# The z projection of a hybrid decoder layer, with its hi products 512 columns wide

## The chip, the cores and the metric

The kernel runs on one core of one Trainium2 chip. The metric is the device time of one execution in microseconds; for the kernel before, three runs gave 731.35, 731.69 and 731.74 us, median 731.69. Differences are read in one further execution that the hardware profiler recorded.

The engines have short names in the profile: PE is the matrix engine (TensorE; PEld is its weight loads), DVE is VectorE, ACT is ScalarE, POOL is GpSimd, SP issues most of the transfers. Each engine takes its instructions in one fixed order and stops at the first one whose inputs are not there. SBUF is the on-chip memory, 128 partitions wide; PSUM is the memory into which PE accumulates, in banks of 128 x 512 float32.

## The reference, cut to what matters

```python
# x: (1, 256, 1024) float32; one layer
h = h + 0.5 * rmsnorm(swiglu(rmsnorm(h, g1), w_gate1, w_up1, w_down1), p1)
u = rmsnorm(h, mix_pre_g)
z, xbc, dt_raw, q, k, v, gate_logits = jnp.split(u @ w_in, IN_SPLITS, axis=-1)   # z: 2048 columns
y_ssd = ssd_branch(z, xbc, dt_raw, ...)      # ... y = y * silu(z), then a grouped rmsnorm and a product
y_att = diff_attn_branch(q, k, v, ...)
h = h + rmsnorm((gates[0] * y_ssd + gates[1] * y_att) @ w_out, mix_post_g)
h = h + 0.5 * rmsnorm(swiglu(rmsnorm(h, g2), w_gate2, w_up2, w_down2), p2)
```

The change touches how `z = u @ w_in[:, 0:2048]` is computed. `z` is needed only at `silu(z)`, after the state-space branch (SSD) has its `y`.

## The kernel before, in words

All products are made in float32r, in which each operand is split into a rounded `hi` part and a rest `lo`, and three of the four partial products are added: hi·hi, hi·lo and lo·hi. The weights stream from HBM in chunks of 1 MB (`raw`, three buffers). For each chunk ACT casts two halves to `whi` (L259) and DVE subtracts to make two halves of `wlo` (L260), two or three chunks ahead of PE.

The normalized input `u` lies transposed in SBUF with 256 tokens: its hi part `ah`, its lo part `al`, and the two side by side in 512 columns as `ahl`.

**The z stage** is the loop at L1517 to L1523. It takes eight weight chunks of 1024 x 256, two for each of four groups g, so `pz00`, `pz01`, `pz10` ... `pz31`; the text below also calls them c0 to c7. For each chunk `mm_t` (L323) writes both 128-row halves m of the result into the two halves of one PSUM bank (`pjt`, of three banks `pj`): per half, 16 matmuls with `whi` as the stationary operand, alternately on `ah` (L330) and `al` (L331), then eight with `wlo` on `ah` (L333), all of 256 columns. Then ACT copies the bank to `sz` (L1522). After the stage ACT applies Silu to `sz`.

The stages next to it (`xs` ahead, `q` and `k` behind) use `mm_w` (L355) on chunks of the same shape. There each half m has a bank of its own: eight matmuls of 512 columns with `whi` on `ahl`, so that hi·hi lands in columns 0 to 255 and hi·lo in 256 to 511, and eight of 256 columns with `wlo` on `ah` into columns 0 to 255 (`mm_part`, L341). Then ACT copies the right half of the bank to SBUF and DVE adds the left one (`taken_from`, L347 and L348).

**Work woven into the z stage.** `back.run(BG_US)` behind each chunk feeds steps of `ssd_work` (L1246). For each group g: PE transposes `xs` (`px`, L1252), DVE scales it to `X` (L1253); for each half hf of the group, a transfer issued on POOL's queue brings the tile `acb` (cumulated decays, broadcast to 128 partitions, L1262); from it ACT and DVE build two tiles `E` (ACT: eight passes over 128 columns and one exp over 512, in the helper `act`, L415; DVE: L1269, and a product with the mask tile, L1274). With all four `E` of a group PE makes `py` (32 matmuls, L1284), in the order 3, 2, 1, 0, so the first `py` matmul needs the last `E`. DVE adds `py` into `xs` (L1291).

**What sets the order.** In this stage no order is written by hand: the framework's scheduler places each engine's instructions at build time from its own estimates, and the chip then keeps that order. POOL's queue holds, around this stage, only the eight `acb` transfers. Buffers: `k4` 29 of 4 KB (weights, `acb`, `sz`), `k2` 7 of 2 KB, `k3` 4 (`E`).

Of the kernel before, what the change touches and what calls it, by code (L numbers as in the profile page):

```python
# [19 lines left out]
ALU = mybir.AluOpType  # L20
# [6 lines left out]
P = 128  # L27
T = 256
# [26 lines left out]
def tile_hybrid_layer(ctx: ExitStack, tc: tile.TileContext, x, ffn1_pre_g, ffn1_w_gate, ffn1_w_up,  # L55
# [4 lines left out]
    nc = tc.nc  # L60
# [5 lines left out]
    def k4(shape, name, dt=F32):  # L66
        return sb.tile(shape, dt, tag="k4", name=name, bufs=K4_BUFS)
# [4 lines left out]
    def k2(shape, name, dt=F32):  # L72
        return sb.tile(shape, dt, tag="k2", name=name, bufs=K2_BUFS)
# [7 lines left out]
    def pj(name):  # L81

        return ps.tile([P, 512], F32, tag="pj", name=name, bufs=3)

    def pjt(name):

        return pj(name).rearrange("p (m t) -> p m t", m=2)

    def bg(shape, name):
        return ps.tile(shape, F32, tag="bg", name=name, bufs=5)  # L90
# [197 lines left out]
    def split_to(n):  # L288

        while len(splits) < min(n, len(units)):  # L290
            of, p = units[len(splits)]
            if p is not None:
                splits.append(of.split(p))
                continue
            for _ in split_steps():
                pass

    def ahead_of(i, n):

        n *= 4  # L300
        while n > 0 and i < len(units):
            n -= 4 if units[i][1] is None else 1
            i += 1
        return i

    def take(ahead=AHEAD):

        i = taken[0]
        taken[0] += 1
        split_to(ahead_of(i, ahead))  # L310
        (of, p), w = units[i], splits[i]
        splits[i] = None
        if p is not None:
            return w
        his, los = w
        nj = chunks[of][1][1] // 2
        return (lambda j: his[j // nj][:, j % nj, :], lambda j: los[j // nj][:, j % nj, :])
# [5 lines left out]
    def mm_t(acc, w, act, k0=0, first=True, last=True, ks=range(KD)):  # L323

        (wh, wl), (ah, al, _) = w, act
        acc = acc if isinstance(acc, list) else [acc[:, m, :] for m in range(2)]
        for m in range(2):
            cs = slice(m * P, (m + 1) * P)
            for j in ks:
                nc.tensor.matmul(acc[m], wh(j)[:, cs], ah(k0 + j), start=first and j == ks[0], stop=False)  # L330
                nc.tensor.matmul(acc[m], wh(j)[:, cs], al(k0 + j), start=False, stop=False)  # L331
            for j in ks:
                nc.tensor.matmul(acc[m], wl(j)[:, cs], ah(k0 + j), start=False, stop=last and j == ks[-1])  # L333

    def mm_part(acc, w, act, m, part, first):


        (wh, wl), (ah, _, ahl) = w, act
        to, w_, x_ = (acc, wh, ahl) if part == "hi" else (acc[:, :T], wl, ah)
        for j in range(KD):  # L340
            nc.tensor.matmul(to, w_(j)[:, m * P:(m + 1) * P], x_(j), start=first and j == 0,  # L341
                             stop=not first and j == KD - 1, skip_group_check=True)

    def taken_from(acc, dst, scale=None):

        if scale is None:
            nc.scalar.copy(dst, acc[:, T:])  # L347
            nc.vector.tensor_tensor(dst, acc[:, :T], dst, ALU.add)  # L348
        else:
            nc.scalar.activation(dst, acc[:, T:], AF.Copy, scale=scale)  # L350
            nc.vector.scalar_tensor_tensor(dst, acc[:, :T], scale, dst, ALU.mult, ALU.add)

    PARTS = (("hi", "lo"), ("lo", "hi"))
# [9 lines left out]
    def mm_runs(dst, name, w, act, n):  # L363


        banks = [pj(f"{name}{m}") if n % 2 == 0 else bg([P, 512], f"{name}{m}") for m in range(2)]
        for part in PARTS[n % 2]:
            for m, acc in enumerate(banks):
                mm_part(acc, w, act, m, part, part == PARTS[n % 2][0])
                if part == PARTS[n % 2][1]:  # L370
                    taken_from(acc, dst[:, m, :])

    def mm_nat(acc, w, act, k0, first, last, late):


        (wh, wl), (ah, al) = w, act
        pairs = [(ah, wh), (al, wh), (ah, wl)] if late == "w" else [(ah, wh), (ah, wl), (al, wh)]
        terms = [(p, j) for j in range(4) for p in pairs[:2]] if late == "w" else \
            [(p, j) for p in pairs[:2] for j in range(4)]
        terms += [(pairs[2], j) for j in range(4)]  # L380
        for i, ((a, b), j) in enumerate(terms):
            nc.tensor.matmul(acc, a(k0 + j), b(j), start=first and i == 0, stop=last and i == 11)  # L382
# [112 lines left out]
    def new_u(tag):  # L495
        for i in range(2):
            uT[i] = sb.tile([P, 4, 2, T], F32R, tag="u8", name=f"u{i}_{tag}", bufs=2)

    act_u = (lambda j: uT[j // 4][:, j % 4, 0, :], lambda j: uT[j // 4][:, j % 4, 1, :],
             lambda j: uT[j // 4][:, j % 4, :, :])  # L500
# [370 lines left out]
    def ffn(post_v, tag, ready, turned, then, products):  # L871
# [28 lines left out]
        for j in range(2, FF // T):  # L900
            if j % 2 == 0:
                gh = k4([P, 4, T], f"gh_{tag}{j}", F32R)
                gl = k4([P, 4, T], f"gl_{tag}{j}", F32R)
            o = (j % 2) * 2
            gu += [(gh[:, o + m, :], gl[:, o + m, :]) for m in range(2)]
            sg = k2([P, 2, T], f"sg_{tag}{j}")
            mm_runs(sg, f"pg_{tag}{j}", take(), act_u, 0)
            act(sg, sg, AF.Silu)
            su = k2([P, 2, T], f"su_{tag}{j}")
            mm_runs(su, f"pup_{tag}{j}", take(), act_u, 1)  # L910
            nc.vector.tensor_tensor(sg, su, sg, ALU.mult)  # L911
            split(gh[:, o:o + 2, :], gl[:, o:o + 2, :], sg)
            if j // 2 in QUADS[tag]:
                if j % 2:
                    sums[j // 2] = sums_of(j // 2, even, sg)
                else:
                    even = sg
# [304 lines left out]
    for i in range(4):  # L1222
        acc = k2([P, 2, T], f"bc{i}")
        mm_w(acc, f"pbc{i}", take(), act_u)
        dst = (bT, cT)[i // 2]
# [16 lines left out]
    sz = [None] * 4  # L1242
# [265 lines left out]
    for g in range(4):  # L1508
        xs[g] = k4([P, 4, T], f"xs{g}")
        for i in range(2):  # L1510
            acc = k2([P, 2, T], f"xr{g}{i}")
# [5 lines left out]
    for g in range(4):  # L1517
        sz[g] = k4([P, 4, T], f"sz{g}")
        for i in range(2):
            acc = pjt(f"pz{g}{i}")  # L1520
            mm_t(acc, take(), act_u)
            nc.scalar.copy(sz[g][:, i * 2:i * 2 + 2, :], acc)  # L1522
            back.run(BG_US)  # L1523
    act_table(SILU)
    for g in range(4):
# [94 lines left out]
    acc = [[bg([P, 512], f"acc_mx{b}{q}") for q in range(2)] for b in range(2)]  # L1620
# [50 lines left out]
```

## Time and profile before

| | |
|---|---|
| median of three runs | 731.69 us |
| the profiled execution | 731.22 us, its span 729.3 us |
| busy, share of the span | PE 99%, PEld 85%, DVE 83%, ACT 65%, POOL 4% |
| xs stage | 237.9 to 285.3 us of the span |
| z stage | 285.3 to 340.0 us |
| q and k stage | 339.9 to 392.0 us |
| `acb` transfers issued on POOL | at 278.59, 284.86, 301.98, 302.94, 317.86, 323.24, 339.79, 346.96 us |

How to read it. The span goes from the first to the last instruction; the profiled execution's own time is 1.92 us longer. A row of a timeline has the start, the duration, engine, line, operation, output<-inputs, shape and count, and in brackets how long the engine stood idle before it and what ended that. Rows of consecutive instructions overlap by some hundredths of a microsecond to a tenth, since the next instruction enters the pipeline before the last one has left; the step from one start to the next is the price in a full queue. Matmuls are pipelined, so that their rows show 0.28 us or 0.39 us for one while the next begins after 0.12 us; the chain of waits shows the step.

### The profile page before, as it was taken

What the parts mean: (1) busy time and instruction counts of PE and PEld (TensorE: products, weight loads), DVE (VectorE), ACT (ScalarE), POOL (GpSimd) and SP (SyncE); (2) the same over time, 40 slices, a digit from 0 to 9 for tenths busy, and PEclk for the clock granted to TensorE, in tenths of its full rate; (3) what the DMA queues carried; (4) which work ended last, traced back from release to release, by engine and by line L of the source; (5) the groups of instructions that cost most, each with busy time, mean ns of one, the idle gap of its engine ahead of it and who ended that gap; (6) DMA issues with size and microseconds to landing.
All of it is one profiled execution on the core that took longest, in us unless ns stands there. A gap on an engine that the chain in (4) does not pass through costs nothing.

```text
span 729.3 us, 10568 instructions
## 1 busy us (share of the span) xinstructions
PE 721.3 (99%) x4025; PEld 620.5 (85%) x4025; DVE 608.5 (83%) x933; ACT 472.8 (65%) x804; POOL 31.5 (4%) x63
## 2 busy tenths in 40 slices
PE   9999999999999999999999999999999999999996
PEld 8888888888778889999888788888888888888885
DVE  6978788999979989777996998785784878789996
ACT  6657666666867676869965577782563756566562
POOL 4300000000200000000000000000010000000000
PEclk9999999999999999999999999999999999999998
DMA  8884654467674557665564664465461655654551
GB/s 303 229 275 153 208 173 176 170 231 260 185 227 119 172 173 238 208 213 180 155 224 147 205 224 137 152 235 199 120 234 51 230 182 166 231 194 156 174 197 58
DMA packets 94450, 137.92 MB, mean 189 GB/s; under 512 B 2668, under 2 KB 68800, under 8 KB 94400
## 3 DMA queue, kind: packets, MB, share of 16 engines
q1 hardware_dynamic: 91728, 129.51, 53.7%
q0 software_dynamic: 2368, 7.22, 3.3%
q8 instruction: 31, 0.51, 0.3%
q10 hardware_dynamic: 304, 0.53, 0.2%
q14 instruction: 19, 0.16, 0.1%
HBM read 136.17 MB, written 1.08 MB: 188 GB/s over the span
## 4 chain that ended last, share of the span: by engine, by line
PE 95%; DVE 2%; DMA 1%; issue 1%; ACT 0%; DVEq 0%; ACTq 0%
PE pup_f L341 14%; PE pg_f L341 14%; PE pxs L341 6%; PE pws L382 6%; PE pgt L382 6%; PE acc_f2p L755 5%; PE acc_f1p L755 3%; PE pbc L341 3%; PE pk L341 3%; PE pq L341 3%; PE pn_f L398 3%; PE acc_mx L676 3%; PE pn_mx L382 3%; PE pn_f L382 3%; PE pwd L382 3%; PE pz L333 2%
## 5 line engine op out<-in xcount | busy, mean ns | idle before, releaser
L260 DVE TENSOR_TENSOR wlo<-raw,whi 128x1024 fp32r<-128x1024 f32 x216 | 257.0, 1219 | 20.2 <-ACT whi L259 19.0
L259 ACT CAST whi<-raw 128x1024 fp32r<-128x1024 f32 x216 | 218.4, 1049 | 16.1 <-DMA raw<-in_w_in_dram 5.7
L341 PE MATMUL pg_f<-u_f,whi 128*128 128x512 f32 x288 | 69.0, 390 | 0.0
L341 PE MATMUL pup_f<-u_f,whi 128*128 128x512 f32 x288 | 68.7, 391 | 0.0
L341 PEld LDWEIGHTS pg_f<-u_f,whi 128*128 128x128 f32 x288 | 53.9, 188 | 11.1
L341 PEld LDWEIGHTS pup_f<-u_f,whi 128*128 128x128 f32 x288 | 52.9, 188 | 10.2
L130 ACT CAST wqh<-wt 128x1024 fp32r<-128x1024 f32 x24 | 25.2, 1055 | 23.5 <-DVE wt L122 23.4
L341 PEld LDWEIGHTS pg_f<-u_f,wlo 128*128 128x128 f32 x288 | 36.9, 191 | 1.4
L341 PE MATMUL pup_f<-u_f,wlo 128*128 128x256 f32 x288 | 37.5, 283 | 0.0
L341 PE MATMUL pg_f<-u_f,wlo 128*128 128x256 f32 x288 | 37.4, 283 | 0.0
L347 ACT COPY su_f<-pup_f 128x256 f32<-128x256 f32 x36 | 13.2, 372 | 36.1 <-PE pup_f L341 36.1
L341 PEld LDWEIGHTS pup_f<-u_f,wlo 128*128 128x128 f32 x288 | 35.9, 192 | 0.0
L348 DVE TENSOR_TENSOR su_f<-pup_f,su_f 128x256 f32<-128x256 f32 x36 | 15.2, 421 | 24.2 <-ACT su_f L347 24.1
L382 PE MATMUL pgt<-whi,u_mx 128*128 128x512 f32 x128 | 33.1, 393 | 0.0
L341 PE MATMUL pxs<-u_mx,whi 128*128 128x512 f32 x128 | 31.8, 394 | 0.0
L330 PE MATMUL pz<-u_mx,whi 128*128 128x256 f32 x128 | 31.6, 284 | 0.0
L331 PE MATMUL pz<-u_mx,whi 128*128 128x256 f32 x128 | 31.5, 283 | 0.0
L136 DVE TENSOR_TENSOR wql<-wt,wqh 128x1024 fp32r<-128x1024 f32 x24 | 29.1, 1217 | 0.2
L382 PEld LDWEIGHTS pgt<-whi,u_mx 128*128 128x128 f32 x128 | 23.6, 188 | 5.3 <-issue 0.7
L341 PEld LDWEIGHTS pxs<-u_mx,whi 128*128 128x128 f32 x128 | 23.2, 189 | 4.3
L320 ACT CAST gh_f<-sg_f 128x512 fp32r<-128x512 f32 x18 | 11.2, 620 | 23.2 <-DVE sg_f L911 23.2
L136 DVE TENSOR_TENSOR wql<-raw,wqh 128x1024 fp32r<-128x1024 f32 x18 | 21.8, 1219 | 3.5 <-ACT wqh L130 3.5
(415 smaller groups left out, 1585.1 us busy)
## 6 DMA issues: line engine op xcount, KB each, us to landing
raw<-in_w_in_dram SPq DMA_DIRECT2D x40, 1024.0 KB, 5.1
raw<-in_ffn_w_down_dram SPq DMA_DIRECT2D x22, 1024.0 KB, 4.9
raw<-in_ffn_w_gate_dram SPq DMA_DIRECT2D x20, 1024.0 KB, 5.4
raw<-in_ffn_w_up_dram SPq DMA_DIRECT2D x20, 1024.0 KB, 5.2
raw<-in_ssd_w_branch_dram SPq DMA_DIRECT2D x8, 1024.0 KB, 5.0
acb<-acd POOLq DMA_DIRECT2D x8, 512.0 KB, 4.1
raw<-in_da_w_branch_dram SPq DMA_DIRECT2D x4, 1024.0 KB, 5.1
raw<-in_w_out_dram SPq DMA_DIRECT2D x4, 1024.0 KB, 5.1
```

Source lines behind the costliest of these rows:

```text
L130: nc.scalar.copy(hi, src)
L136: nc.vector.tensor_sub(lo, src, hi.bitcast(F32))
L259: last_cast[0] = behind(nc.scalar.copy(hi, r[:, js, :]), "cast").ins
L260: m = nc.vector.tensor_sub(lo, r[:, js, :], hi.bitcast(F32))
L330: nc.tensor.matmul(acc[m], wh(j)[:, cs], ah(k0 + j), start=first and j == ks[0], stop=False)
L331: nc.tensor.matmul(acc[m], wh(j)[:, cs], al(k0 + j), start=False, stop=False)
L341: nc.tensor.matmul(to, w_(j)[:, m * P:(m + 1) * P], x_(j), start=first and j == 0, stop=not first and j == KD - 1, skip_group_check=True)
L348: nc.vector.tensor_tensor(dst, acc[:, :T], dst, ALU.add)
L382: nc.tensor.matmul(acc, a(k0 + j), b(j), start=first and i == 0, stop=last and i == 11)
L398: nc.tensor.matmul(accs[b], x_(k0 + j), w_(j), start=first and j == 0 and w_ is wh and x_ is acts[b][0], stop=last and j == 3 and w_ is wl)
L676: nc.tensor.matmul(acc[b][q][:, cs] if to is None else to, x_[:, ts], w_(kt)[:, halves[q]][:, cs], start=to is not None and kt == 0 and x_ ...
L755: nc.tensor.matmul(bank[p], x_, w_, start=p not in begun, stop=last and p in (1, 5, 6, 7))
```

## The change

`mm_folded` replaces `mm_t` in the z stage. The products take the form of the neighbouring stages: per half m a bank of its own, eight matmuls of 512 columns with `whi` and eight of 256 with `wlo`. ACT copies the whole bank of 512 columns into an SBUF tile `both` (from `k2`), once per half, so twice per chunk. The sum of the two halves of `both`, 256 columns, is made by GpSimd, out of SBUF into `sz`: 16 additions in the stage.

```diff
+    def mm_folded(dst, name, w, act):
+        for m in range(2):
+            acc = pj(f"{name}{m}")
+            for part in PARTS[m]:
+                mm_part(acc, w, act, m, part, part == PARTS[m][0])
+            both = k2([P, 512], f"{name}b{m}")
+            nc.scalar.copy(both, acc)
+            nc.gpsimd.tensor_tensor(dst[:, m, :], both[:, :T], both[:, T:], ALU.add)
...
     for g in range(4):
         sz[g] = k4([P, 4, T], f"sz{g}")
         for i in range(2):
-            acc = pjt(f"pz{g}{i}")
-            mm_t(acc, take(), act_u)
-            nc.scalar.copy(sz[g][:, i * 2:i * 2 + 2, :], acc)
+            mm_folded(sz[g][:, i * 2:i * 2 + 2, :], f"pz{g}{i}", take(), act_u)
             back.run(BG_US)
```

In the rows below, `acb10` is the transfer for group 1, half 0, `sz1<-pz11b0` the addition for group 1, second chunk, half m = 0. POOL's queue from the second to the sixth `acb` transfer, before:

```order
L1262 DMA acb01_3052<-acd_2146 128x1024
L1262 DMA acb10_3228<-acd_2146 128x1024
L1262 DMA acb11_3248<-acd_2146 128x1024
L1262 DMA acb20_3424<-acd_2146 128x1024
L1262 DMA acb21_3505<-acd_2146 128x1024
```

And with the change, from the addition of the second chunk's second half on:

```order
L382 TENSOR_TENSOR sz0_2898<-pz01b1_3029 128x256
L382 TENSOR_TENSOR sz1_3052<-pz10b0_3080 128x256
L382 TENSOR_TENSOR sz1_3052<-pz10b1_3100 128x256
L382 TENSOR_TENSOR sz1_3052<-pz11b0_3165 128x256
L1273 DMA acb10_3188<-acd_2146 128x1024
L382 TENSOR_TENSOR sz1_3052<-pz11b1_3185 128x256
L1273 DMA acb11_3208<-acd_2146 128x1024
L382 TENSOR_TENSOR sz2_3219<-pz20b0_3247 128x256
L382 TENSOR_TENSOR sz2_3219<-pz20b1_3267 128x256
L382 TENSOR_TENSOR sz2_3219<-pz21b0_3328 128x256
L382 TENSOR_TENSOR sz2_3219<-pz21b1_3348 128x256
L1273 DMA acb20_3364<-acd_2146 128x1024
```

`acb10` now stands behind the addition of chunk c3's first half, `acb11` behind that of its second, `acb20` behind all four of group 2. Further on, `acb21` stands behind the addition of c6's first half and `acb30` behind the last one; at the front, `acb00` stands behind the addition of c0's first half.

ACT's queue at the `E` tiles of group 1 (`whi` are casts of coming weights), before:

```order
L1522 COPY sz1_3072<-pz11_3168 128x512
L259 COPY whi551_3265<-raw55_3001 128x1024
L415 ACTIVATE E100_3230<-acb10_3228,acs_2145 128x128 x4
L415 ACTIVATE E100_3230<-E100_3230 128x2x256
L415 ACTIVATE E101_3239<-acb10_3228,acs_2145 128x128 x4
L415 ACTIVATE E101_3239<-E101_3239 128x2x256
L415 ACTIVATE E110_3250<-acb11_3248,acs_2145 128x128 x4
L415 ACTIVATE E110_3250<-E110_3250 128x2x256
L1522 COPY sz2_3259<-pz20_3260 128x512
L415 ACTIVATE E111_3320<-acb11_3248,acs_2145 128x128 x4
L415 ACTIVATE E111_3320<-E111_3320 128x2x256
```

And with the change:

```order
L381 COPY pz11b1_3185<-pz111_3168 128x512
L259 COPY whi550_3220<-raw55_2990 128x1024
L259 COPY whi551_3224<-raw55_2990 128x1024
L426 ACTIVATE E100_3190<-acb10_3188,acs_2145 128x128 x4
L426 ACTIVATE E100_3190<-E100_3190 128x2x256
L426 ACTIVATE E101_3199<-acb10_3188,acs_2145 128x128 x4
L426 ACTIVATE E101_3199<-E101_3199 128x2x256
L426 ACTIVATE E110_3210<-acb11_3208,acs_2145 128x128 x4
L426 ACTIVATE E110_3210<-E110_3210 128x2x256
L381 COPY pz20b0_3247<-pz200_3230 128x512
L381 COPY pz20b1_3267<-pz201_3250 128x512
L426 ACTIVATE E111_3270<-acb11_3208,acs_2145 128x128 x4
```

A second cast and a second copy stand between the copy of chunk c3 and the end of `E111`. On PE, `py` of group 0 stands 13 matmuls of 256 columns into c3 before, and eight of 512 and three of 256 into it now; `py` of group 1 stands seven matmuls ahead of c5's end before, and two of 512 columns into c6 now; `py` of group 2 stands behind seven matmuls of `pq01` (256 columns each) before, and behind its eight of 256 and three of 512 now.

## The prediction

> **What bounds the kernel now.** I read the chain of waits first: who sets the end.
>
> ```profile
> PE 95%; DVE 2%; DMA 1%; issue 1%; ACT 0%; DVEq 0%; ACTq 0%
> ```
>
> PE sets it almost alone. The stage table then says how close the others are behind it in the z stage (busy time of PE, PEld, DVE, ACT, POOL; granted clock; DMA share):
>
> ```profile
> 285.30:340.00 54.70, 54.70 (x474) 52.93 (x473) 43.96 (x74) 41.31 (x84) 2.43 (x6) 1.00 0.65 203
> ```
>
> PE is busy all the 54.7 us, at clock 1.00. DVE has 10.7 us spare and ACT 13.4, POOL does nothing but issue transfers. Spare time is not slack, though: PE needs the last `E` tile of a group before its `py`. Three views of that, the chain (start, length, work), then ACT's and DVE's timelines around the `E` tiles of group 1, and the last `E` product of group 0:
>
> ```profile
> 305.15 2.75 PE py L1284 x32
> 307.91 1.02 PE px L1252 x8
> 323.80 2.75 PE py L1284 x32
> 343.60 2.75 PE py L1284 x32
> ```
>
> ```profile
> 313.16 0.59 ACT L1522 COPY sz<-pz 128x512 f32<-128x512 f32 x1 [5.06 <-PE pz L333]
> 313.65 1.05 ACT L259 CAST whi<-raw 128x1024 fp32r<-128x1024 f32 x1
> 314.59 1.28 ACT L415 ACTIVATE E<-acb,acs 128x128 f32<-128x128 f32 x4
> 316.30 1.27 ACT L415 ACTIVATE E<-acb,acs 128x128 f32<-128x128 f32 x4
> 321.85 1.99 ACT L259 CAST whi<-raw 128x1024 fp32r<-128x1024 f32 x2
> 321.99 0.96 DVE L1274 TENSOR_TENSOR E<-E,cbm 128x768 f32<-128x768 f32 x1 [1.22 <-ACT E L415]
> 303.88 0.96 DVE L1274 TENSOR_TENSOR E<-E,cbm 128x768 f32<-128x768 f32 x1 [0.74 <-ACT E L415]
> ```
>
> Group 1's last `E` is ready at 322.95 and PE starts `py` at 323.80: 0.85 us to spare. Group 0's is ready at 304.84 for 305.15: 0.3 us. ACT waits for PE's bank (5.06 us) and then runs the whole way to the last `E` without a pause, so what is put into that stretch, or delays its start, reaches PE almost at once.
>
> **What the change removes.** The two forms of a chunk stand in the chain, the xs stage's and z's:
>
> ```profile
> 244.43 5.59 PE pxs L341 x32
> 285.70 0.12 PE pz L330
> 287.38 0.96 PE pz L333 x8
> ```
>
> z now: 48 steps of 0.12 = 5.76 us. The new form, with the same shapes as `pxs`: 5.59 us, of which 16 x 0.12 are the `wlo` products, so a step of 512 columns is 0.229 us. Saved: 0.17 x 8 = **-1.4 us**, all of it on PE. More there cannot be: as many columns stream as before. PE's weight loads fall by 128, beside it.
>
> **What it adds on ACT.** Eight copies more of 128x512: from the first row of ACT above to the next is 0.49 us, together 3.9 us, against 13.4 spare. In group 1's stretch the order now has two casts and two copies where one of each stood. From the rows: copy to cast 0.49, cast to `E` 0.94, one `E` pair to the next 1.71, last exp to the end of DVE's product 322.95 - 321.85 = 1.1.
>
> **What it adds on POOL, and this decides.** The `acb` transfers that feed the `E` tiles now queue behind additions. What does an addition cost? No GpSimd operation on two wide tiles is in the trace. The nearest are these, with DVE's rows at the same moments:
>
> ```profile
> 190.56 2.91 POOL L570 TENSOR_SCALAR dr_mx<-ident,r_mx 128x128 f32<-128x128 f32 x1
> 190.58 0.67 DVE L605 TENSOR_TENSOR og_f<-c_f,pg_f 128x512 f32<-128x512 f32 x1
> 191.18 1.21 DVE L260 TENSOR_TENSOR wlo<-raw,whi 128x1024 fp32r<-128x1024 f32 x1
> 192.31 1.44 DVE L645 SCALAR_TENSOR_TENSOR h<-og_f,rp_f,h 128x512 f32<-128x512 f32 x2
> 548.92 0.79 POOL L570 TENSOR_SCALAR dr_f<-ident,r_f 128x128 f32<-128x128 f32 x1
> 548.97 1.03 DVE L565 TENSOR_SCALAR un_f<-h,r_f 128x512 f32<-128x512 f32 x2 [1.89 <-POOL r_f L512]
> 539.15 0.56 POOL L512 TENSOR_TENSOR r_f<-r_f,small 128x1 f32<-128x1 f32 x1
> 189.49 0.30 POOL L511 TENSOR_SCALAR r_mx<-ss_mx 128x1 f32<-128x1 f32 x1 [22.40 <-ACT sq_mx L506]
> ```
>
> One and the same line of POOL took 0.79 us beside a DVE that reads one SBUF tile, and 2.91 us beside a DVE that ran, without a gap, operations on two SBUF tiles each. It was not a cold start: another TENSOR_SCALAR had just run in 0.30. DVE's rows beside the long one are as long as elsewhere (`wlo` 1.21). So POOL pays for the collision, DVE does not.
>
> Undisturbed, an addition over 256 columns lies between 0.56 us (the one-column row) and 0.56 + 2 x (0.79 - 0.30) = 1.54; I take 1.1. Disturbed, it lies between that 1.1 (no collision) and 1.54 x 2.91/0.79 = 5.7; I take a = **3.0 us**, near the one disturbed row, which is half as wide but wholly covered. The z stage disturbs much:
>
> ```profile
> L260 DVE TENSOR_TENSOR wlo<-raw,whi 128x1024 fp32r<-128x1024 f32 x18 | 21.4, 1218 | 2.3 <-ACT whi L259 2.3
> L1274 DVE TENSOR_TENSOR E<-E,cbm 128x768 f32<-128x768 f32 x10 | 9.6, 956 | 5.8 <-ACT E L415 5.8
> 309.94 3.48 DVE L260 TENSOR_TENSOR wlo<-raw,whi 128x1024 fp32r<-128x1024 f32 x3
> ```
>
> Both groups read two SBUF tiles: 31 of 54.7 us. The third row, three casts' rests in a row, is what meets the addition ahead of `acb10`.
>
> The Trainium skill (SBUF — State Buffer, section "SBUF: two separate sides") says that VectorE, when it reads two SBUF inputs, and a GpSimd operation that reads SBUF exclude each other, and that whichever starts first holds the ports while the other is blocked for its whole instruction. Here POOL started 0.02 us ahead of DVE and DVE was not blocked, so of this rule the trace bears out the collision but not who pays; what the rule would make of the time is the third rival.
>
> **The steps on PE's path.** From issue to landing a transfer takes 4.1:
>
> ```profile
> DMA to landing us min/median/max: 3.6/4.1/5.9
> ```
>
> *py of group 1*, counted from the start of group 0's `py`. PE: 2.75 + 1.02 + five `wlo` steps 0.6 = 4.4, c3's first half is done; second half 2.8, so 7.2; c4 and c5 11.2; two steps of 512 0.46: it is at `py` at 18.8. ACT: c3's second copy is done at 7.2 + 0.1 + 0.5, two casts 1.9: ready for `E` at 9.7. POOL: c3's first copy done at 5.0, the addition a, landing 4.1: `acb10` is there at 9.1 + a = 12.1. From there four `E` pairs 6.84, two copies 0.98, the last product 1.1: 21.0. PE stands still for **2.2 us** (a - 0.8; at a = 1.1 it is 0.3). A `pj` bank that waits for c4's copy behind `E110` is late inside the same wait.
>
> *py of group 0.* The start of its chain:
>
> ```profile
> 285.30 0.28 PE L330 MATMUL pz<-u_mx,whi 128*128 128x256 f32 x1
> 291.21 0.63 ACT L415 ACTIVATE xs<-xs 128x512 f32<-128x512 f32 x1 [3.08 <-DVE xs L1200]
> 291.86 1.28 ACT L408 ACT_TABLE_LOAD   x1
> 293.15 0.59 ACT L1522 COPY sz<-pz 128x512 f32<-128x512 f32 x1
> ```
>
> PE comes to `py` at 285.30 + 5.59 + 0.9 (`px`) + 11.18 + 2.19 = 305.1, as before. ACT: c0's second copy ends at 291.5, then Silu 0.65, table 1.29, two casts: 295.3. c0's first half ends at 288.1, its copy at 288.7; with a and 4.1 `acb00` lands at 295.8. Then 6.84 + 0.98 + one cast 0.95 + 1.1 = 9.9: 305.7. PE stands still for **0.6 us** (a - 2.4, at least 0.1).
>
> *py of group 2*, from the start of group 1's. DVE's work behind `py`, and ACT's first `E` of group 3:
>
> ```profile
> L1291 DVE SCALAR_TENSOR_TENSOR xs<-xs,cols_b,py 128x256 f32<-128x256 f32 x8 | 3.5, 476 | 1.5 <-PE py L1284 1.5
> L1253 DVE TENSOR_TENSOR X<-px,dt 128x512 f32<-128x512 f32 x6 | 3.9, 684 | 1.2 <-PE px L1252 1.2
> 353.41 1.28 ACT L415 ACTIVATE E<-acb,acs 128x128 f32<-128x128 f32 x4
> ```
>
> PE: `py` and `px` 3.7, the rest of c6's first half 2.3 (together 6.0), its second half 2.8, c7 5.6, `pq00` 2.8, and of `pq01` eight steps of 0.12 and three of 0.229: 18.9. POOL: c4's copies end 3.3 and 2.8 us ahead of this `py` (one `E` pair and a product lie behind them), two disturbed additions bring it to 2.7; c5's two fall beside the first two rows above, which read one SBUF tile each, so 1.1 apiece: 4.9, and `acb20` lands at 9.0. ACT would be ready at 7.6 (c6's first half 6.0, a copy, a cast). `E200`, c6's other copy and `E201` last to 12.9; `acb21`, behind c6's addition (6.6 + a), lands at 13.7; `E210`, a cast, two copies, `E211` and the product: 20.1. PE stands still for **1.2 us** (nothing at a = 1.1).
>
> Group 3's first transfer, behind the last addition, lands some 7 us after group 2's `py`; its first `E` stood 9.8 us after it (343.60 to 353.41), so nothing there. `sz` is read by Silu after all this, and a `both` buffer comes up again after six other tiles: both free as long as POOL lags by less than three chunks, 17 us.
>
> **The sum:** -1.4 + 0.6 + 2.2 + 1.2 = +2.6 us. On the profiled execution's 731.22 (span 729.3 and 1.92 around it) that is 733.8; the median of the runs is 0.47 higher, so I predict **734.3 us**, slower by 0.36%.
>
> **Rivals.**
>
> *Short additions.* If POOL is hardly disturbed (a = 1.1), the three waits are 0.1, 0.3 and 0: -1.4 + 0.4 = -1.0, 730.7. For it: one disturbed row is thin evidence, and the disturbing is only 31 of 54.7 us. Against it: it is the same engine beside the very `wlo` rows. This is the side "not slower"; it turns at about a = 1.9, where the waits (0.1, 1.1, some 0.2) eat the saving.
>
> *All waits hidden.* -1.4, 730.3. It needs group 0's 0.3 us of spare to hold with a copy more; chance small.
>
> *DVE pays.* An addition holds DVE up for 1.1 us: the conv that precedes Silu is 1.1 later and c1's two additions outrun the group's idle, so `py` of group 0 some 2.0; two additions before `E111` against 1.22 idle (DVE's row above), 1.0 + 0.3; group 2 about 1.0: 4.3 - 1.4 = +2.9, 734.6. Against it: DVE's undelayed rows at 190.58 to 192.31. It is the case in which the Trainium skill's rule (SBUF — State Buffer, "SBUF: two separate sides") would hold with the additions in front.
>
> *POOL falls behind.* At a = 4, c4's to c6's additions queue up on each other: waits 1.6, 3.2 and 4.4, less 1.4 = +7.8, 739.5. For it: an addition reads four times what the 2.91 us row read. Against it: while DVE waits for `acb`, POOL is undisturbed and catches up.
>
> That the change does not do what it says is excluded for PE: `pxs` already shows the price.
>
> **Chances and range.** Forecast 0.42, DVE pays 0.14, POOL falls behind 0.14: slower 0.70. Short additions 0.24: inside 0.2%, which is 1.46 us and about what a measurement of this kernel can tell from no change. All hidden 0.06: -1.4 is at that edge, and I count it as faster. So faster 0.06, same 0.24. The range reaches from short additions, 730.6, to near POOL falling behind, 739.0; the forecast's own (a from 2.2 to 3.4, waits 2.0 to 5.7) is 732.3 to 736.0.
>
> **What would show it.** PE's `pz` steps of 0.229 us and 5.6 a chunk: else the first term is wrong. POOL's additions around 3 us beside `wlo` and about 1 us beside `py`: if all are near 1, short additions. Idle time of PE ahead of `py`, ended by DVE's `E`, itself behind ACT's `E` that waits for `acb`: if ACT never waits for `acb`, the forecast's mechanism is wrong; if `wlo` rows grow beyond 1.22, DVE pays. PE idle at other places (banks `pj`, `wlo`) would be something that I have not priced.

## The result, and the profile after

The change makes the kernel slower: 739.51 us (median of 4 runs, 739.18 to 739.91) beside 731.52 us before (4 runs, 730.93 to 731.74), a ratio of 1.0115 with a 95% interval of 1.0102 to 1.0127. The direction forecast is right. The time lies 0.5 us above the predicted range and 5.2 us above the forecast. The profiled execution took 739.64 us, its span is 737.9 us, 8.6 more than before.

The chain of waits of the changed kernel, by engine:

```profile
PE 77%; issue 7%; ACT 5%; DVE 5%; DMA 4%; POOL 1%; SPq 0%; DVEq 0%; POOLq 0%; ACTq 0%
```

PE set 95% of the chain before. Now transfers, ACT and DVE have a larger part in it, and GpSimd's additions stand in it too. The table by stage (length; busy time of PE, PEld, DVE, ACT, POOL; granted clock; DMA share; GB/s) shows where:

```profile
285.30:349.00 63.70, 60.08 (x374) 51.23 (x372) 47.25 (x74) 47.14 (x98) 18.77 (x22) 0.97 0.56 182
349.00:401.00 52.00, 48.64 (x309) 41.37 (x309) 44.85 (x70) 38.56 (x67) 1.72 (x4) 1.00 0.67 212
```

Both stages are no longer full on PE, and in the first the clock is 0.97. To compare runs I measure one stretch, from the first `pz` matmul to the first matmul of the gates (`pgt`): 285.30 to 391.67 us before, 106.37 long, and 285.72 to 400.35 after, 114.63 long. The difference is 8.26 us. Ahead of the stretch the two executions differ by 0.42 us, which is scatter (it begins between 284.1 and 286.0 us in the runs below), and behind it by less than that.

PE's timeline of the changed kernel, around each place where it stands (start, duration, count, and in brackets the idle time before the row and what ended it):

```profile
305.40 0.51 PE L341 MATMUL pz<-u_mx,wlo 128*128 128x256 f32 x3
306.52 2.82 PE L1295 MATMUL py<-E,X 128*64 128x256 f32 x32 [0.61 <-DVE E L1285]
...
320.98 1.11 PE L341 MATMUL pz<-u_mx,wlo 128*128 128x256 f32 x8
325.08 1.43 PE L341 MATMUL pz<-u_mx,wlo 128*128 128x256 f32 x8 [2.99 <-ACT pz20b L381]
326.30 3.87 PE L341 MATMUL pz<-u_mx,whi 128*128 128x512 f32 x10
330.10 2.82 PE L1295 MATMUL py<-E,X 128*64 128x256 f32 x32
...
348.26 0.86 PE L341 MATMUL pq<-u_mx,whi 128*128 128x512 f32 x3
350.30 2.82 PE L1295 MATMUL py<-E,X 128*64 128x256 f32 x32 [1.19 <-DVE E L1285]
...
357.04 1.11 PE L341 MATMUL pk<-u_mx,wlo 128*128 128x256 f32 x8
359.62 1.22 PE L341 MATMUL pk<-u_mx,wlo 128*128 128x256 f32 x8 [1.48 <-DVE q L351]
...
369.90 1.11 PE L341 MATMUL pk<-u_mx,wlo 128*128 128x256 f32 x8
371.71 1.21 PE L341 MATMUL pk<-u_mx,wlo 128*128 128x256 f32 x8 [0.70 <-DVE q L351]
```

From these rows the loss at each place is the next row's start, less the steps of 0.12 us (256 columns) and 0.229 us (512 columns) that lie between:

| place | working | lost |
|---|---|---|
| `py` of group 0 | 306.52 - 305.40 - 3 x 0.12 | 0.76 |
| bank for c5's second half | 325.08 - 320.98 - 8 x 0.12 | 3.14 |
| the 18 matmuls behind that stop | 330.10 - 325.08 - 8 x 0.12 - 10 x 0.229 | 1.77 |
| `py` of group 2 | 350.30 - 348.26 - 3 x 0.229 | 1.35 |
| banks in the q and k stage | 359.62 - 357.04 - 0.96, and 371.71 - 369.90 - 0.96 | 1.62 + 0.85 |

Together 9.5 us. Less the saving on PE, which an experiment below measures at 1.48, that is 8.0 of the 8.26 us. Of the rest, a tenth lies behind each of the two stops at `pk`, where the next eight steps of 0.12 us took 1.06 and 1.05 us. `py` of group 1 at 330.10 waits for nothing any more: the bank ahead of it took the whole delay.

What the bank waits for: first the transfer, from the chain of the same execution (start, length, work), then two rows of ACT's timeline:

```profile
315.16 7.58 DMA acb<-acd
```

```profile
322.76 1.28 ACT L426 ACTIVATE E<-acb,acs 128x128 f32<-128x128 f32 x4 [1.88 <-DMA acb<-acd]
324.46 1.04 ACT L381 COPY pz20b<-pz 128x512 f32<-128x512 f32 x2
```

`acb11` lands 7.58 us after its issue. ACT, which stands at `E110`, starts at 322.76, and only then gets to the copies of c4. The first of the two, of 0.57 us, frees PE's bank, and PE goes on at 325.08. GpSimd's timeline says why the transfer left so late:

```profile
311.72 1.47 POOL L382 TENSOR_TENSOR sz<-pz11b 128x256 f32<-128x256 f32 x1 [2.77 <-ACT pz11b L381]
313.14 0.57 POOL L1273 DMA_DIRECT2D acb<-acd  x1
314.48 0.73 POOL L382 TENSOR_TENSOR sz<-pz11b 128x256 f32<-128x256 f32 x1 [0.77 <-ACT pz11b L381]
315.16 0.57 POOL L1273 DMA_DIRECT2D acb<-acd  x1
```

GpSimd is idle ahead of both additions, 2.77 and 0.77 us: each waits for ACT's copy of c3, and the transfer waits behind it. Before, the two transfers left at 301.98 and 302.94, 3.2 and 2.2 us ahead of group 0's `py`; now they leave 6.6 and 8.6 us behind it. The additions themselves take 1.47 and 0.73 us.

### The profile page after: what moved, and what is told of

Same layout as the page of the kernel before. It is cut to its first block, busy times and chain, and to the rows that moved or that the text cites. A ratio compares the mean times of both kernels' runs of the same rounds, so it can differ in the third digit from the quotient of the medians.

```text
span 737.9 us, 10347 instructions
## 1 busy us (share of the span) xinstructions
PE 722.6 (98%) x3897; PEld 614.6 (83%) x3897; DVE 611.6 (83%) x933; ACT 477.0 (65%) x812; POOL 46.6 (6%) x79
## 4 chain that ended last, share of the span: by engine, by line
PE 77%; issue 7%; ACT 5%; DVE 5%; DMA 4%; POOL 1%; SPq 0%; DVEq 0%; POOLq 0%; ACTq 0%
PE pup_f L341 14%; PE pg_f L341 14%; PE pws L393 6%; PE pgt L393 6%; PE acc_f2p L766 5%; PE pbc L341 3%; PE acc_mx L687 3%; PE pn_mx L393 3%; PE pn_f L393 3%; PE pwd L393 3%; PE pn_f L409 3%; DMA acb<-acd 3%; ACT E L426 2%; PE pk L341 2%; PE pxs L341 2%
## 5 line engine op out<-in xcount | busy, mean ns | idle before, releaser
L341 PE MATMUL pz<-u_mx,whi 128*128 128x512 f32 x128 | 32.7, 406 | 0.0
L341 PEld LDWEIGHTS pz<-u_mx,whi 128*128 128x128 f32 x128 | 24.5, 197 | 4.9
```

## The experiments

Each is timed against the kernel before on the same chip; a ratio stands with its 95% interval. "Stretch" is the one defined above (106.37 before, 114.63 with the change).

### Additions left out

```diff
-            nc.gpsimd.tensor_tensor(dst[:, m, :], both[:, :T], both[:, T:], ALU.add)
...
+        nc.gpsimd.memset(sz[g], 1.0)
```

> The 16 GpSimd additions are left out (sz is filled with ones by one memset per group, so z itself is not computed); PE's products, ScalarE's 16 whole-bank copies and the use of the banks stay as in the change. Theory (the acb transfers are late because POOL's queue has them behind additions that wait for ScalarE's copies): acb is issued early again, ScalarE does not wait for it, PE's new form shows its saving: 730.0 to 731.2 us, PE idle in the z stage under 1 us. Rival 1 (eight copies more on ScalarE, and two of three banks taken per chunk, delay the chain to py): nothing of that is removed, 737 to 740 us. Rival 2 (GpSimd's reads slow VectorE down): wlo rows back to 1.22, time 730 to 731.5 too, so this run does not tell it from the theory; the acb issue times do.

Measured: 732.76 us, ratio 1.0030 (1.0017 to 1.0043), stretch 108.01. `acb10` and `acb11` leave at 299.82 and 300.68, and ACT waits for no `acb`. So the additions carry most of the loss, but the time misses the theory's range: the kernel is still slower than before. PE's waits in this run (total, times, longest):

```profile
PE pk L341 <- DVE q L351: 2.5, 2, 1.8
```

There is no addition in this kernel that could cause this wait. It is a second cause, which the prediction does not have.

### Additions on VectorE

```diff
-            nc.gpsimd.tensor_tensor(dst[:, m, :], both[:, :T], both[:, T:], ALU.add)
+            nc.vector.tensor_tensor(dst[:, m, :], both[:, :T], both[:, T:], ALU.add)
```

> The additions run on VectorE, out of the same SBUF copies, instead of GpSimd. POOL's queue holds transfers alone, as before. Theory: 730.2 to 732.5 us; VectorE has 16 x 0.42 = 6.7 us more in a stage with 10.7 us spare, which may cost up to 2 us at the py matmuls. Rival 1 (copies and banks): 737 to 740 us. If VectorE cannot bear it: above 733 with idle PE behind VectorE's wlo or E rows.

Measured: 732.15 us, ratio 1.0018 (1.0009 to 1.0028), stretch 107.78; `acb10` and `acb11` leave together at 301.72, and PE's wait at `pk` is 2.2 us. The additions as work are nearly free even on the fuller engine. What costs is where they stand on GpSimd.

### The old products with additions on GpSimd

```diff
-            nc.scalar.copy(sz[g][:, i * 2:i * 2 + 2, :], acc)
+            both = k2([P, 2, T], f"pz{g}{i}b")
+            nc.scalar.copy(both, acc)
+            for m in range(2):
+                nc.gpsimd.tensor_tensor(sz[g][:, i * 2 + m, :], both[:, m, :], both[:, 1 - m, :], ALU.add)
```

> The products of before (256 columns, one bank and one ScalarE copy per chunk), but the copy goes to an SBUF tile and GpSimd makes two additions of 256 columns out of it (of the two halves with each other, so sz is not z). POOL's queue has the additions ahead of acb as in the change; ScalarE's load, PE's products and the banks are those of before. Theory: the loss comes back without the change's products: 736 to 742 us, acb issued after 310 us for group 1 and ScalarE waiting for it. Rival 1 (copies and banks): 731 to 732.5 us.

Measured: 738.26 us, ratio 1.0103 (1.0085 to 1.0121), stretch 113.96. ACT's waits:

```profile
ACT E L415 <- DMA acb<-acd: 10.7, 4, 6.1
```

The stretch is 7.6 us longer than before. In the change it is 8.3 us longer, or 9.7 us without the 1.48 that its products save. Neither the products of 512 columns nor the extra copies are in this kernel, so additions on GpSimd ahead of the transfers are enough by themselves for most of the loss.

### The neighbouring stages' form

```diff
-            mm_folded(sz[g][:, i * 2:i * 2 + 2, :], f"pz{g}{i}", take(), act_u)
+            mm_w(sz[g][:, i * 2:i * 2 + 2, :], f"pz{g}{i}", take(), act_u)
```

> z in the very form of its neighbour stages: two banks, ScalarE copies only the right half (256 columns), VectorE adds the left half from PSUM. POOL as before. Theory: 730.2 to 732 us: PE's 1.4 us saved, ScalarE 16 x 0.37 = 6.0 us against 4.7 us before, VectorE 6.7 us more. Rival 1 in its part on the banks: 733 or more, since two of three banks are in use here too.

Measured: 730.50 us, ratio 0.9992 (0.9983 to 1.0001), stretch 105.83. ACT copies 256 columns instead of 512, DVE adds, GpSimd does nothing but transfers; no wait at `pk`. The wide products are not what loses time, but of the 1.4 us that they save only 0.5 arrive.

### Additions on GpSimd, placed behind the transfers

```diff
-            nc.gpsimd.tensor_tensor(dst[:, m, :], both[:, :T], both[:, T:], ALU.add)
+            held_adds.append((dst[:, m, :], both))
...
-                nc.gpsimd.dma_start(acb, acd[r0:r0 + 4, :].partition_broadcast(P))
+                last_acb[0] = nc.gpsimd.dma_start(acb, acd[r0:r0 + 4, :].partition_broadcast(P))
...
+    def add_held(keep):
+        while len(held_adds) > keep:
+            d, both = held_adds.pop(0)
+            a = nc.gpsimd.tensor_tensor(d, both[:, :T], both[:, T:], ALU.add)
+            if last_acb[0] is not None:
+                tc.add_manual_dep(a.ins, last_acb[0].ins.name, order, reason="behind acb")
...
             back.run(BG_US)
+            add_held(2)
+    add_held(0)
```

> Everything of the change is kept, GpSimd's 16 additions too; only POOL's queue is reordered: each chunk's additions are handed out one chunk later and pinned behind the last acb transfer then known, so that both transfers of a group stand ahead of the additions that they stood behind. Theory (order of POOL's queue): acb10 is issued about 305 us instead of 313.1, ScalarE no longer waits for acb, 730.5 to 733 us, like the two runs without GpSimd additions. Rival 2 (the additions themselves do the harm, by colliding with VectorE's reads or with the transfers): 736 us or more, with wlo rows above 1.25 or landing times near 6 us though acb is issued early.

Measured: 732.65 us, ratio 1.0026 (1.0016 to 1.0035), stretch 108.21. The same 16 additions run on the same engine. GpSimd's issues of `acb10` and `acb11` in this run:

```profile
300.80 1.10 POOL L1275 DMA_DIRECT2D acb<-acd  x2
```

They are 12 and 14 us earlier than in the changed kernel, and ACT waits for no `acb`. Placing the additions behind the transfers takes 6.4 of the 8.3 us away.

With the additions handed out without delay (`add_held(0)` behind each chunk), but still pinned behind the last transfer:

> As the run before, but the additions are not held a chunk back: acb10 and acb11 stand behind c2's additions instead of c3's, acb20 behind c4's instead of c5's. A half dose of the suspected cause. Theory: between, 732 to 736 us. Rival 2: as the change, 738 to 740 us.

Measured: 732.32 us, ratio 1.0019 (1.0009 to 1.0028), stretch 107.66. Here `acb10` and `acb11` leave at 307.86, later than in the run above, and ACT still does not wait. So it did not need the full distance; it was expected up to 736 and is as good as the other.

### The transfers on SP's queue

```diff
-                nc.gpsimd.dma_start(acb, acd[r0:r0 + 4, :].partition_broadcast(P))
+                nc.sync.dma_start(acb, acd[r0:r0 + 4, :].partition_broadcast(P))
```

> The additions stay on GpSimd as in the change; the acb transfers are issued from SP's queue, among the weight loads, instead of POOL's. Theory: nothing of acb waits for an addition, 731 to 735 us (a transfer can now wait behind a weight load that waits for its buffer, or hold one up). Rival 2: 736 us or more.

Measured: 737.49 us, ratio 1.0093 (1.0078 to 1.0108), stretch 112.50. The theory missed, and the time lies where the rival, harm by the additions themselves, was expected; but the two versions above, with all 16 additions on GpSimd, speak against that rival. No addition stands ahead of the transfers now, but weight loads do: the last two leave at 354.44, where the kernel before issues its last two at 339.79 and 346.96. The tile view of `acb`, and behind it ACT's waits:

```profile
DMA to landing us min/median/max: 6.0/6.5/7.4
```

```profile
ACT E L426 <- DMA acb<-acd: 3.9, 4, 2.2
```

The transfers are late again, and in the chain of this run two of them, issued at 328.79 and 354.44, stand ahead of the `q` for which PE stops at `pk`. GpSimd's queue is a bad place for them only with additions in it; on SP's they are no better off.

### The second cause: the Silu block and q's banks

In the version with the additions behind the transfers, PE waits at `pk` for a bank that DVE's addition of `q` frees. ACT's and DVE's rows in the timeline there, behind the Silu block:

```profile
348.23 2.00 ACT L259 CAST whi<-raw 128x1024 fp32r<-128x1024 f32 x2
349.56 2.35 DVE L260 TENSOR_TENSOR wlo<-raw,whi 128x1024 fp32r<-128x1024 f32 x2
350.13 0.65 ACT L350 ACTIVATE q<-pq 128x256 f32<-128x256 f32 x2
351.83 0.75 DVE L351 SCALAR_TENSOR_TENSOR q<-pq,q 128x256 f32<-128x256 f32 x2
```

And in the kernel before:

```profile
348.81 1.05 ACT L259 CAST whi<-raw 128x1024 fp32r<-128x1024 f32 x1
349.76 0.65 ACT L350 ACTIVATE q<-pq 128x256 f32<-128x256 f32 x2
349.89 1.23 DVE L260 TENSOR_TENSOR wlo<-raw,whi 128x1024 fp32r<-128x1024 f32 x1
351.03 0.75 DVE L351 SCALAR_TENSOR_TENSOR q<-pq,q 128x256 f32<-128x256 f32 x2
```

Behind the Silu block ACT has two casts where it had one, so DVE has two `wlo` ahead of `q` instead of one. `q` comes 0.8 us later, while PE, with its shorter products, starts `pk` 1.6 us earlier (347.51 and 349.13). What counts is how far `q` comes behind the start of `pk`. It is 1.90 us in the kernel before and 2.27 in the neighbouring form, which has two casts there too, and PE does not stand. It is 3.46 with the old products and additions, 4.05 with the change and 4.32 in the version above, and PE's first stop at `pk` is 0.90, 1.48 and 1.75 us: each time 2.6 less, so in these runs a distance under 2.6 us costs nothing. The version with the old products has one cast there, but its whole Silu block starts 5.6 us later than in the kernel before, behind late `E` tiles (347.88 and 342.31), so the first cause feeds the second. To test whether the block is what holds the bank up, the Silu block is handed out one chunk later (the additions still behind the transfers):

```diff
-    act_table(SILU)
-    for g in range(4):
-        act(sz[g], sz[g], AF.Silu)
-    act_table(EXP_LN)
-    back.add(ssd_norm(range(4)))
...
         mm_w(qT[c // 2][:, o:o + 2, :], f"pq{c}", take(), act_u, 0.125)
+        if c == 0:
+            act_table(SILU)
+            for g in range(4):
+                act(sz[g], sz[g], AF.Silu)
+            act_table(EXP_LN)
+            back.add(ssd_norm(range(4)))
```

> The additions stay on GpSimd behind the acb transfers as in the pinned version, and the Silu block (two table loads, four Silu) is handed out one q chunk later, so that the two casts of the next weight chunk come ahead of it or into it and DVE has no pair of wlo rows between the Silu-dependent work and the q additions. Theory (the rest of the loss, 1.8 us over before, is one pj bank that the q additions free late, because the eight wider copies on ACT pushed a cast behind the Silu block): PE's wait at pk for q falls from 2.5 us to under 0.5, and the time from 732.65 to 730.2 to 731.0, under or at the kernel before. Rival (the rest is the additions themselves, that disturb DVE and the transfers all over the z stage): the wait moves to another place of the same stage and the time stays at 732.2 to 733.

Measured: 730.00 us beside 730.22, ratio 0.9992 (0.9983 to 1.0001), stretch 105.77. All of PE's waits in the two stages:

```profile
PE pq L341 <- DVE k L348: 0.3, 1, 0.3
PE py L1297 <- DVE E L1287: 0.2, 1, 0.2
```

The wait at `pk` is gone and 2.4 us of the stretch with it. The same arithmetic as the change, in another order, is level with the kernel before.

With the four Silu and their table loads left out instead:

> The pinned version with the four Silu and their two table loads left out (sz goes into the product without Silu), so that ACT has 6.5 us less to do between the last z copy and the first q copy. Theory (late bank behind the Silu block): no wait of PE at pk, and 729.8 to 730.8. Rival (the additions themselves): the bank wait goes, but 1.0 to 1.8 us of PE's idle time stays elsewhere in the z and q stages: 731.5 to 732.5.

Measured: 730.85 us, ratio 0.9999 (0.9990 to 1.0008), stretch 106.19. No wait at `pk`; one of 0.8 us appears at `pq`, for ACT's last `z` copy. Most of the theory holds, though the time is a little above its range, and less is won than by moving the block. The copy is late because ACT works without a pause from 333.75 us on until it ends, with `E` tiles and casts ahead of it in the queue.

### Was the 2.91 us row a first use?

```diff
     nc.gpsimd.memset(ones, 1.0)
+    nc.gpsimd.tensor_scalar(m3[:, 0, :], ident, ones[:, 0:1], None, ALU.mult)
```

> The changed kernel with one more GpSimd instruction at its very start, the same form as the 2.91 us row (TENSOR_SCALAR on 128x128 float32, ident times a column), long before anything else runs on GpSimd beside DVE. If the 2.91 us were a collision with DVE's two-input rows, as the prediction took it, the row dr_mx stays at 2.7 to 2.9 us. If they were the first use of that form of instruction, the new row takes about 2.9 us (or 0.8 plus what the first use costs) and dr_mx falls to 0.8 to 1.1. The time of the whole: 739 to 740 in both cases.

One execution: 740.47 us. GpSimd's timeline has the added instruction at the start, then the row that the prediction used:

```profile
1.64 0.62 POOL L480 TENSOR_SCALAR m<-ident,ones 128x128 f32<-128x128 f32 x1
...
190.42 2.91 POOL L582 TENSOR_SCALAR dr_mx<-ident,r_mx 128x128 f32<-128x128 f32 x1
```

The first use costs nothing, and the row stays at 2.91 us. That it is a collision with DVE's rows, as the prediction took it, other runs show. In the kernel before it starts 0.02 us ahead of DVE's `og_f` row and takes 2.91 us; without the additions it starts 0.13 us behind that row and takes 2.77; with the late Silu block 0.50 behind, and takes 2.40. In all three it ends 2.9 us after `og_f` began, so its end hangs on DVE's rows and not on its own start. What was wrong was to take it as the price of an addition.

### Transfers handed out one group earlier

```diff
+        def fetch(g):
+            for hf in range(2):
+                acbs[g, hf] = acb = k4([P, 4, T], f"acb{g}{hf}")
+                r0 = g * 8 + hf * 4
+                nc.gpsimd.dma_start(acb, acd[r0:r0 + 4, :].partition_broadcast(P))
+        fetch(0)
...
-                acb = k4([P, 4, T], f"acb{g}{hf}")
+                acb = acbs.pop((g, hf))
...
+            if g < 3:
+                fetch(g + 1)
             py = [bg([P, 2, T], f"py{g}{hf}") for hf in range(2)]
```

First in the changed kernel, with the later Silu block and no pin:

> The changed kernel with its additions on GpSimd in their own places, without any pin, but both acb transfers of a group issued one group earlier (ahead of the py products of the group before), and the Silu block one q chunk later. Theory (of the 8 us all is lost by two things: transfers that stand behind additions and land too late for their group, and one bank that is freed late behind the Silu block): each acb is there some 10 us before its E, no wait of ACT for acb, no wait of PE at pk, and 729.5 to 730.5, at or under the kernel before, although the additions still stand ahead of the transfers in GpSimd's queue. Rival (additions between weight loads and transfers cost time of their own, so that only keeping them behind the transfers helps): 731.5 to 734, with PE waiting for E or for banks in the z stage.

Measured: 740.79 us, ratio 1.0127 (1.0107 to 1.0146), stretch 117.35: both expectations missed, and the worst of all runs. GpSimd's timeline:

```profile
307.62 1.30 POOL L382 TENSOR_TENSOR sz<-pz10b 128x256 f32<-128x256 f32 x1 [3.26 <-ACT pz10b L381]
308.86 0.57 POOL L1264 DMA_DIRECT2D acb<-acd  x1
...
339.45 4.45 POOL L382 TENSOR_TENSOR sz<-pz30b 128x256 f32<-128x256 f32 x1 [1.89 <-ACT pz30b L381]
```

The program hands the transfers out earlier, but the scheduler again put an addition that waits for ACT ahead of `acb10`; it left at 308.86 where pinning gave 300.80. And one addition alone took 4.45 us ahead of group 3's transfers.

Then in the neighbouring stages' form, with the Silu block where it was:

> The neighbouring stages' form for z (ACT copies the right half, DVE adds the left one; no addition on GpSimd) with the acb transfers one group earlier and the Silu block where it was. It is to tell whether the 1.4 us that PE saves can be had: theory (PE's saving is real and is given back where E or a bank comes late): 729.3 to 730.3 beside 730.2 to 730.9 for the kernel before, a ratio of 0.998 to 0.9995. Rival (the saving is lost further on whatever is done, as weights arrive no earlier): the same as the kernel before within 0.1%.

Measured: 728.78 us beside 731.55, ratio 0.9965 (0.9953 to 0.9978): faster than both kernels, and better than the range. (The profiled spans differ by 1.8 us, the medians by 2.8; the interval begins at 1.6.) The stage table over the z and most of the q and k stage:

```profile
285.30:400.00 114.70, 114.70 (x721) 98.62 (x720) 101.27 (x172) 89.56 (x172) 3.69 (x7) 1.00 0.61 192
```

PE has no gap, and the stretch is 104.89 us, 1.48 less than before: the saving on PE is real and can be had whole. GpSimd's timeline has group 1's transfers (group 0's leave together at 277.56):

```profile
295.15 1.05 POOL L1264 DMA_DIRECT2D acb<-acd  x2 [16.34 <-PE pz L341]
```

In the neighbouring form alone `acb10` and `acb11` leave at 301.29, so here, with no addition in GpSimd's queue, handing them out earlier did bring them 6 us forward. ACT starts on group 1's `E` at 305.88 and not at 314.85, and PE's stop of 0.45 us for a bank that DVE frees, which the neighbouring form has at 321.42, is gone. The order of the `E` tiles on ACT and DVE changed with the transfers; which of the two removes that stop was not separated.

## Why the prediction was off

**What held.** PE bound the kernel; the products save 8 x 0.17 = 1.4 us (1.48 in the last run). The `acb` transfers come late behind the additions, ACT waits for them, and PE stands ahead of `py`: the forecast's mechanism. That the change could not be worth more than 1.4 us on PE held too.

Two of the three waits came out near their price: `py` of group 0 was priced at 0.6 and lost 0.76, `py` of group 2 at 1.2 and lost 1.35. That was luck. The sum had 3.0 for the addition and 4.1 for the landing, 7.1 together. At group 0 the addition took 1.07 and `acb00` landed after 6.3, 7.4 together; at group 2 they took 0.86 and 5.97 (`acb21`), 6.8 together. Two wrong sizes cancelled.

**The price of an addition, a = 3.0 us, was wrong.** Two of the changed kernel's rows by tile (count, shortest/median/longest in ns):

```profile
L382 POOL TENSOR_TENSOR sz<-pz11b x2: 731/1100/1470, 311.7 to 314.5; 128x256 f32<-128x256 f32 x2
L382 POOL TENSOR_TENSOR sz<-pz21b x2: 1203/1248/1294, 328.7 to 330.5; 128x256 f32<-128x256 f32 x2
```

All sixteen lie between 0.73 and 1.47 us, near the 1.1 that the prediction gave to an undisturbed one. By its own sum that is the rival "short additions", 730.7 us, "not slower"; measured were 739.5. So the quantity on which the prediction let everything turn, a, does not decide. What does is the place in GpSimd's queue: were the addition ahead of `acb11` free, its transfer would leave 0.7 us earlier, against the 10.8 us by which it is late relative to `py` of group 0. The sum did count that wait (copy, addition, landing), but gave all uncertainty to a, and none to the other two terms.

**The landing of 4.1 us was wrong, and half the clock was missing.** The tile view of `acb` after the change:

```profile
DMA to landing us min/median/max: 3.8/5.8/7.6
```

With the issue later, the transfers fall among weight loads: two of 1 MB, issued between 312 and 324 us beside `acb10` and `acb11`, themselves took 8.0 us to land, where the median of such loads is 5.1. In the sum for `py` of group 1 `acb10` decided; by the same numbers `acb11` would leave 11.0 us after group 0's `py` began and land at 15.1, in time for its `E` at 12.1 + 2 x 1.71 = 15.5. It left earlier, after 8.6 us, and landed later, after 16.2, so the wait now sat at `E110` and then at PE's bank. The prediction had called a late bank "late inside the same wait", and it was: without it PE would have come to `py` at 325.19, and the last `E` product ended at 328.20. So this wait is 3.14 us where 2.2 were priced. The other 1.77 us at group 1 are the slow matmuls behind the stop. The prediction had PE at full clock throughout and no term for this; it is shown below.

**"So nothing there" for group 3, and the eight copies "against 13.4 spare", were wrong.** The banks of the q and k stage lost 2.5 us. The step from the last `z` copies over the Silu block to the banks of `q` was not followed: there ACT has no spare time, whatever it has over the stage, and an earlier PE only waits longer. Moving the block one chunk on removes the loss. That the extra copies alone cause it is not shown: the version with the old products has none, and stands there too. The prediction had named idle banks as something "not priced"; that is where it went.

Group 1, 4.9 us where 2.2 were priced, and the banks, 2.5 where nothing was, make up 5.2 of the 6.0 us by which the profiled span grew beyond the sum (8.6 where the sum has 2.6). The rest is 0.3 at the other two `py`, 0.4 ahead of the stretch, and tenths.

**The rivals.** "POOL falls behind" gives the right time, 739.5, by a mechanism that did not occur, so that is luck as well: GpSimd is idle ahead of most additions. "DVE pays" is partly borne out, below, and does not make up the loss: with the additions on GpSimd but behind the transfers, the version of 730.0 us has them all.

## What to carry to other kernels

An instruction that is put into a queue costs what it waits for, not only what it takes: ask of each what stands behind it, and when its own input is there. On an engine that also issues transfers, place the transfers first by an explicit order; handing them out earlier in the program was not enough here, where a scheduler put additions ahead of them again. And an engine's spare time over a stage says nothing of its last microseconds: follow what a few extra instructions push behind the next long block.

## What the hardware showed that was not expected

**After some stops PE runs at half clock.** The table by microsecond behind the stop of 2.99 us (columns as above; the clock is the third number from the end):

```profile
326.00:327.00 1.00, 1.00 (x5) 0.91 (x4) 0.00 (x0) 1.00 (x4) 0.83 (x2) 0.50 0.04 13
...
328.00:329.00 1.00, 1.00 (x4) 0.80 (x3) 1.00 (x2) 1.00 (x3) 0.30 (x1) 0.50 0.00 0
329.00:330.00 1.00, 1.00 (x5) 0.59 (x3) 0.80 (x2) 0.77 (x2) 0.99 (x1) 0.84 0.00 0
```

From about 325.9 to 329.3 the clock is 0.50, and ten matmuls of 512 columns take 3.80 us where 2.29 are usual: a stop of 3.1 us cost 1.8 more. The old products with additions show the same behind 2.23 us of idle time, the early transfers in the changed kernel behind 1.89 and behind 2.00. Each time the half clock lasts 3.4 us. With the transfers on SP's queue, PE does not slow down behind a longer stop:

```profile
354.34 1.23 PE L341 MATMUL pk<-u_mx,wlo 128*128 128x256 f32 x8 [2.86 <-DVE q L351]
355.40 2.00 PE L341 MATMUL pk<-u_mx,whi 128*128 128x512 f32 x8
```

So the length of the stop alone does not decide. The Trainium skill (TensorE: Matmul & The Clock Gate, section "Part 1: The HAM clock gate") says that a gate judges PE's activity by free-running windows of about 3.4 us, halves the clock after an idle one and restores it after a busy one. The half clock and its 3.4 us agree with this, and so does it that stops of like length differ. Its rule that idle gaps above about 3.4 us are the ones to avoid does not: gaps of 1.89 to 2.99 us were enough here, and none of them fills such a window.

**Additions and DVE delay each other.** The addition of 1.47 us above began while DVE was in the first of these two rows of the changed kernel; the second row is the same pair with GpSimd idle:

```profile
311.38 2.89 DVE L260 TENSOR_TENSOR wlo<-raw,whi 128x1024 fp32r<-128x1024 f32 x2
...
356.87 2.36 DVE L260 TENSOR_TENSOR wlo<-raw,whi 128x1024 fp32r<-128x1024 f32 x2
```

The addition takes 0.74 us more than the shortest one and the pair of `wlo` 0.53 us more, as if GpSimd waited for the running `wlo` and then DVE for the addition. Not always: the addition of 4.45 us in the run with early transfers began 0.04 us ahead of these rows, and ended 0.6 us after the last of them:

```profile
339.49 1.81 DVE L1293 TENSOR_TENSOR E<-E,cbm 128x768 f32<-128x768 f32 x2
341.22 1.21 DVE L260 TENSOR_TENSOR wlo<-raw,whi 128x1024 fp32r<-128x1024 f32 x1
342.36 0.95 DVE L1293 TENSOR_TENSOR E<-E,cbm 128x768 f32<-128x768 f32 x1
```

Four instructions passed it. The 2.91 us row stood in the same way behind DVE rows that followed each other without a gap. The prediction's "POOL pays for the collision, DVE does not" holds for these two rows, not for the pair above. The Trainium skill (SBUF — State Buffer, section "SBUF: two separate sides") has whichever starts first hold the ports for its whole instruction: the 0.53 us of DVE agree with it, four DVE instructions ahead of an addition that stood as begun do not, unless the start of GpSimd's row is earlier than the moment at which it took the ports, which the profile does not show. What decides whether GpSimd gets its turn between two rows stays open.
